# Contiguous halves instead of interleaved chunks of rows in a row-normalising kernel

## The chip, the cores and the metric

One core of a Trainium2 chip; the other cores are idle. The metric is device microseconds (us) of one execution. "Span" is the time from the first to the last instruction in the profile; the time metric lies some 1.7 to 1.8 us above it. Engines: VectorE (DVE), ScalarE (ACT), GpSimd (POOL), SyncE (SP, which here only issues DMAs), and 16 DMA engines that carry every transfer.

## The reference

```python
# x: [1024, 4096] float32, axis = -1, eps = 1e-12
norm = np.sqrt(np.sum(x ** 2, axis=axis, keepdims=True) + eps)
return (x / norm).astype(np.float32)
```

Each row is divided by its own length. A row is 16 KiB, the tensor 16.78 MB; it is read once and written once. No row depends on another, so the kernel is free to give any row to any partition.

## The kernel before

Two tiles, each 128 partitions x 4 rows x 4096 floats (64 KiB per partition, 8.39 MB in all). Both loads are issued at once, then each tile is squared and summed, scaled in place and stored. All four DMAs go through SP's queue.

```python
R = 4
n_tiles = N // (P * R)                       # 2
x_t = x.rearrange("(p t r) d -> t p (r d)", t=n_tiles, r=R)
out_t = out_flat.rearrange("(p t r) d -> t p (r d)", t=n_tiles, r=R)
...
for i in range(n_tiles):
    ...
    load = nc.sync.dma_start(out=g.flat(), in_=x_t[i])
    ...
for i, g in enumerate(groups):
    g.square_dve(R - 1)          # sum of squares of row 3 on VectorE
    g.square_act(0)              # of row 0 on ScalarE
    g.norm(0)                    # sqrt on ScalarE, reciprocal on VectorE
    g.scale(0)                   # x *= 1/norm on VectorE
    ...
    store = nc.sync.dma_start(out=out_t[i], in_=g.flat())
```

Partition p holds rows 8p to 8p+7: rows 8p..8p+3 in tile 0 and rows 8p+4..8p+7 in tile 1. In either tile a partition's four rows are one contiguous run of 64 KiB in HBM, and the runs of neighbouring partitions begin 128 KiB apart.

Of the kernel before, what the change touches and what calls it, by code (L numbers as in the profile page):

```python
# [82 lines left out]
def first_load_to_front(nc, load):  # L83






    def move(program):  # L90
        blocks = program.main_func.blocks
        entry = blocks[0].instructions
        if any(i.name == load.name for i in entry):
            return
        body = next(
            b.instructions
            for b in blocks
            if any(i.name == load.name for i in b.instructions)
        )
        at = next(n for n, i in enumerate(body) if i.name == load.name)  # L100
        assert not body[at].sync_info.on_wait
        before = next(
            n
            for n, i in enumerate(entry)
            if i.engine == mybir.EngineType.SP and isinstance(i, mybir.InstDrain)
        )
        entry.insert(before, body.pop(at))

    nc.at_finalize(move)
# [72 lines left out]
@with_exitstack  # L182
def kernel(
    ctx: ExitStack,
    tc: tile.TileContext,
    x: bass.AP,
    axis: bass.AP,
    eps: bass.AP,
    out: bass.AP,
):  # L190
    nc = tc.nc
    P = nc.NUM_PARTITIONS

    assert isinstance(axis, int) and axis in (-1, len(x.shape) - 1)
    eps = float(eps)

    x = x.flatten_outer_dims()
    out_flat = out.flatten_outer_dims()
    N, D = x.shape
    R = 4  # L200
    assert N % (P * R) == 0
    n_tiles = N // (P * R)
    x_t = x.rearrange("(p t r) d -> t p (r d)", t=n_tiles, r=R)
    out_t = out_flat.rearrange("(p t r) d -> t p (r d)", t=n_tiles, r=R)

    io = ctx.enter_context(tc.tile_pool(name="io", bufs=n_tiles))
    scratch_pool = ctx.enter_context(tc.tile_pool(name="scratch", bufs=1))
    stats = ctx.enter_context(tc.tile_pool(name="stats", bufs=n_tiles))

    eps_t = scratch_pool.tile([P, 1], F32)  # L210
    nc.vector.memset(eps_t, eps)  # L211
    sq_act = scratch_pool.tile([P, D], F32)
    sq_dve = scratch_pool.tile([P, D], F32)
    scratch = {"act": sq_act, "dve": sq_dve}

    groups = []
    for i in range(n_tiles):
        g = RowGroups(nc, io, stats, scratch, D, R, eps_t)
        load = nc.sync.dma_start(out=g.flat(), in_=x_t[i])
        if i == 0:  # L220
            first_load_to_front(nc, load.ins)
        groups.append(g)

    for i, g in enumerate(groups):
        g.square_dve(R - 1)
        g.square_act(0)
        g.norm(0)
        g.scale(0)
        g.square_act(1)
        g.norm(1)  # L230
        g.norm(R - 1)
        g.scale(1)
        g.scale(R - 1)
        g.square_act(2)
        g.norm(2)
        if i < n_tiles - 1:
            g.scale_by_both(2)
        else:
            g.scale(2)
        store = nc.sync.dma_start(out=out_t[i], in_=g.flat())  # L240
    gpsimd_waits_for_last_store(nc, store.ins)
# [35 lines left out]
```

## Time and profile before

| | before |
|---|---|
| time, median of 3 runs | 81.94 us (81.75 to 81.99) |
| span in the profile | 80.2 us |
| DVE / ACT busy | 26.7 / 29.7 us |
| DMA packets | 512 of 64 KiB, 64 completion signals |
| first and second load landed | 22.08 / 41.40 us |

The lines behind the table are shown in the prediction.

### The profile page before, as it was taken

The numbers are of one execution on the slowest core, as the hardware profiler recorded it, in microseconds if no ns is written. First come the engines' busy times: TensorE is split into PE (matmuls) and PEld (weight loads), VectorE is DVE, ScalarE is ACT, GpSimd is POOL, SyncE is SP. The second block draws the span as 40 slices with busy tenths as digits, with TensorE's granted clock in tenths as the row PEclk, the third lists the DMA queues.
The fourth block names the chain that finished last, engine by engine and source line by source line (L and its number), as shares of the span: only waits on it lengthen the run. The fifth ranks groups of instructions, "written<-read, shape, count | busy, mean of one in ns | idle before, by whom it ended". The sixth has DMA issues, their size and how long they took to land.

```text
span 80.2 us, 93 instructions
## 1 busy us (share of the span) xinstructions
DVE 26.7 (33%) x21; ACT 29.7 (37%) x23; POOL 0.2 (0%) x4
## 2 busy tenths in 40 slices
DVE  0000000000099599960039995999200000000000
ACT  6000000000099999989439999950000000000000
POOL 0000000000000000000000000000000000000000
DMA  9099996699996699996699990999991999992990
GB/s 490 33 523 523 523 490 294 261 523 523 523 490 261 294 523 523 523 490 261 294 523 523 523 490 33 523 523 523 523 458 65 523 523 523 523 425 98 523 523 0
DMA packets 576, 33.55 MB, mean 418 GB/s; under 512 B 64, under 2 KB 64, under 8 KB 64
## 3 DMA queue, kind: packets, MB, share of 16 engines
q1 hardware_dynamic: 576, 33.55, 97.4%
HBM read 16.78 MB, written 16.78 MB: 418 GB/s over the span
## 4 chain that ended last, share of the span: by engine, by line
DMA 51%; ACT 10%; DVE 9%; issue 0%
DMA xt<-in_x_dram 51%; ACT sq_act L33 9%; DVE xt L64 9%; ACT rstd L53 1%; DVE rstd L59 0%
## 5 line engine op out<-in xcount | busy, mean ns | idle before, releaser
L33 ACT ACTIVATE sq_act<-xt 128x4096 f32<-128x4096 f32 x6 | 21.7, 3609 | 22.4 <-DMA xt<-in_x_dram 22.4
L42 DVE SCALAR_TENSOR_TENSOR sq_dve<-xt 128x4096 f32<-128x4096 f32 x2 | 8.9, 4426 | 26.4 <-DMA xt<-in_x_dram 26.4
L64 DVE TENSOR_SCALAR xt<-xt,rstd 128x4096 f32<-128x4096 f32 x7 | 16.5, 2353 | 0.2
L72 ACT ACTIVATE xt<-xt,rstd 128x3584 f32<-128x3584 f32 x1 | 3.3, 3283 | 0.2 <-DVE rstd L59 0.2
L53 ACT ACTIVATE rstd<-ssq,eps_t 128x1 f32<-128x1 f32 x8 | 2.1, 290 | 0.1
L59 DVE RECIPROCAL rstd<-rstd 128x1 f32<-128x1 f32 x8 | 1.3, 160 | 2.5 <-ACT rstd L53 2.5
L33 ACT ACT_TABLE_LOAD x1 | 1.3, 1283 | 0.8 <-PEq L258 0.8
L53 ACT ACT_TABLE_LOAD x1 | 1.3, 1283 | 0.0
L33 ACT ACTIVATION_READ_ACCUMULATOR sq_act<-xt 128x1 f32 x6 | 1.1, 187 | 0.0
L78 DVE TENSOR_SCALAR xt<-xt,rstd 128x512 f32<-128x512 f32 x1 | 0.5, 487 | 0.0
L211 DVE MEMSET eps_t<- 128x1 f32 x1 | 0.1, 59 | 0.9 <-PEq L258 0.9
L42 DVE DVE_READ_ACCUMULATOR sq_dve<-xt 128x1 f32 x2 | 0.2, 83 | 0.0
L258 POOL MEMSET const-uint8-127<- 128x1 uint8 x1 | 0.1, 103 | 0.0
L258 POOL MEMSET const-bfloat16-1.0<- 128x1 bf16 x1 | 0.1, 102 | 0.0
L258 POOL MEMSET const-float32-0.0<- 128x1 f32 x1 | 0.1, 99 | 0.2 <-issue 0.2
L258 POOL MEMSET const-float32-1.0<- 128x1 f32 x1 | 0.1, 99 | 0.0
## 6 DMA issues: line engine op xcount, KB each, us to landing
xt<-in_x_dram SPq DMA_DIRECT2D x2, 31.3
out_dram<-xt SPq DMA_DIRECT2D x2, 22.5
```

Of the source, the lines that this page charges most:

```text
L33: self.nc.scalar.activation(out=sq_a, in_=self.x[:, r], func=ACT_F.Square, accum_out=self.ssq[:, r : r + 1],)
L42: self.nc.vector.scalar_tensor_tensor(out=sq_v, in0=self.x[:, r], scalar=1.0, in1=self.x[:, r], op0=ALU.mult, op1=ALU.mult, accum_out=self ...
L53: self.nc.scalar.activation(out=self.rstd[:, r : r + n], in_=self.ssq[:, r : r + n], func=ACT_F.Sqrt, bias=self.eps_t,)
L59: self.nc.vector.reciprocal(out=self.rstd[:, r : r + n], in_=self.rstd[:, r : r + n])
L64: self.nc.vector.tensor_scalar_mul(out=self.x[:, r], in0=self.x[:, r], scalar1=self.rstd[:, r : r + 1])
L72: self.nc.scalar.activation(out=self.x[:, r, :cut], in_=self.x[:, r, :cut], func=ACT_F.Copy, scale=rstd,)
L78: self.nc.vector.tensor_scalar_mul(out=self.x[:, r, cut:], in0=self.x[:, r, cut:], scalar1=rstd)
L211: nc.vector.memset(eps_t, eps)
L258: nc = _bacc.Bacc("TRN2", target_bir_lowering=False, num_devices=1)
```

## The change

The intent, as far as the edit shows it: each tile becomes one contiguous 8 MiB half of the tensor, so that a load or store walks through HBM without leaving every second 64 KiB out.

```diff
-    x_t = x.rearrange("(p t r) d -> t p (r d)", t=n_tiles, r=R)
-    out_t = out_flat.rearrange("(p t r) d -> t p (r d)", t=n_tiles, r=R)
+    x_t = x.rearrange("(t p r) d -> t p (r d)", p=P, r=R)
+    out_t = out_flat.rearrange("(t p r) d -> t p (r d)", p=P, r=R)
```

That is the whole diff. Partition p now holds rows 4p..4p+3 in tile 0 and rows 512+4p..512+4p+3 in tile 1.

## The prediction

> **What bounds the kernel now.** I start with the page of the kernel before: busy engines, the slices, the queue and the chain that ended last.
>
> ```profile
> DVE 26.7 (33%) x21; ACT 29.7 (37%) x23; POOL 0.2 (0%) x4
> ...
> DMA packets 576, 33.55 MB, mean 418 GB/s; under 512 B 64, under 2 KB 64, under 8 KB 64
> ...
> q1 hardware_dynamic: 576, 33.55, 97.4%
> ...
> DMA 51%; ACT 10%; DVE 9%; issue 0%
> ```
>
> VectorE and ScalarE are busy for a third of the 80.2 us span, while packets on the 16 DMA engines fill 97.4% of it. 576 packets are 512 large ones plus 64 tiny ones (the "under 512 B" count): 33,554,432 bytes / 512 = 65,536 bytes, so each large packet is exactly one partition's four rows of 16 KiB. The 64 tiny ones are 16 for each of the four transfers, which are the completion signals. The row of tenths in the slices, with its sixes and zeros, should not be read as idle DMA: a packet takes longer than a 2 us slice, so whole packets fall into one slice or the next. The chain of waits says DMA 51% only, but it ends at the last compute instruction (54.38 + 2.35 = 56.7 us), not at the last store. So it does not show what sets the end. The timeline does:
>
> ```profile
> 0.00 1.12 SPq L219 DMA_DIRECT2D xt<-in_x_dram  x2
> ...
> 22.08 3.62 ACT L33 ACTIVATE sq_act<-xt 128x4096 f32<-128x4096 f32 x1 [20.01 <-DMA xt<-in_x_dram]
> ...
> 38.99 18.11 SPq L240 DMA_DIRECT2D out_dram<-xt  x2
> 41.40 3.62 ACT L33 ACTIVATE sq_act<-xt 128x4096 f32<-128x4096 f32 x1 [2.43 <-DMA xt<-in_x_dram]
> ```
>
> Load 1 has landed at 22.08 us and load 2 at 41.40. The two loads lie in one queue one behind the other, so the second one alone cost 41.40 - 22.08 = 19.32 us for 8,388,608 bytes: 434 GB/s. The stores were issued at 38.99 and about 56.8 us. The view of the output tensor gives their times to landing:
>
> ```profile
> DMA to landing us min/median/max: 21.7/22.5/23.3
> ```
>
> That puts them at 38.99 + 21.7 = 60.7 and 56.8 + 23.3 = 80.1 us. The four landings are at 22.1, 41.4, 60.7 and 80.1, evenly 19.3 us apart: loads and stores cost the same, and nothing lies between them. Windows cut where each transfer ends confirm it (columns: stretch in us, its length, busy time of DVE, ACT, POOL, clock, DMA share, GB/s):
>
> ```profile
> 1.00:20.66 19.66, 0.00 (x0) 1.07 (x1) 0.00 (x0) 1.00 1.02 427
> 20.66:40.00 19.34, 12.45 (x10) 16.56 (x12) 0.00 (x0) 1.00 1.00 434
> 40.00:59.35 19.35, 14.23 (x10) 11.88 (x10) 0.00 (x0) 1.00 1.00 434
> 59.35:78.70 19.35, 0.00 (x0) 0.00 (x0) 0.00 (x0) 1.00 1.00 434
> ```
>
> So the span is one DMA pipe: about 1.0 us before the first packet, then 78.7 - 1.0 = 77.7 us of packets, then 80.2 - 78.7 = 1.5 us until the last completion is seen and the program ends. The packet records say the same from below: nearly all large packets take 2.42 us, each engine moves 32 of them, 32 x 2.42 = 77.4 us. Only the first packet of each engine is longer, 2.4 to 3.4 us with a mean of 3.07: 0.65 us of start-up. The time outside the span is 81.94 - 80.2 = 1.7 us (the profiled execution itself took 82.04), and the change cannot touch it.
>
> **What the Trainium skill says.** "DMA: Bandwidth & Descriptors", section "Where 436 GB/s comes from", puts the ceiling of the 16 engines' SBUF ports at 435.2 GB/s (16 ports x 32 B x 850 MHz). The trace agrees closely: 434 GB/s in three windows, 99.7% of it. "HBM Reference", section "Specifications (TRN2)", has a domain at about 716 GB/s, and adds that a core streaming alone is bounded by its 16 engines; the equal speed of loads and stores fits that, though no run so far measures HBM by itself. Against the change stands a row of the first page, section "Latency and other measured facts", on HBM row pitch at large powers of two: tiles of 128 x 16 KiB copied between HBM tensors made 207 GB/s at a pitch of 512 KiB, 164 at 2 MiB and 103 at 4 MiB, against 214 for a padded pitch. The kernel before has a pitch of 128 KiB between partitions and shows no loss at all; the change halves the pitch, which is the harmless direction of that row. Last, the same page's "Why a DMA increments its semaphore by 16 and not by 1" says the slowest dimension of both patterns decides the number of engines, and 128 gives 16; the 16 completions per transfer in the page above agree.
>
> **The change, part by part.** Only two address patterns change. I built both kernels and compared instruction order: every engine has the same rows (DVE 21, ACT 17, SP 5), with the same waits. In the built program each of the four transfers is, on the HBM side, 128 runs of 16,384 floats; the step from one run to the next goes from 32,768 floats (128 KiB) to 16,384 (64 KiB), and the second tile's offset from 64 KiB to 8 MiB. The SBUF side is untouched.
>
> - Removed: nothing. Added: nothing. Compute is 0 us of difference: the reductions go over one row whichever row it is.
> - Bytes: 2 x 16.78 MB both ways, difference 0.
> - Packets: still 128 runs of 65,536 bytes per transfer. The run was already contiguous, because a partition's four rows lie together in both layouts. So contiguity of the whole tile joins no packets, as a packet cannot cross from one SBUF partition to another. 512 x 0 us saved.
> - Speed of a packet: at 434 of 435.2 GB/s (a figure of the skill) the most that a friendlier HBM order could give is 77.4 x 0.3% = 0.2 us (estimate). The start-up could give at most its 0.65 us. The whole upside is under 0.9 us, 1.1%.
> - Compute overlap: from landing 1 to the issue of store 1 it is 38.99 - 22.08 = 16.9 us, against 19.3 us of load 2. Store 1 is thus queued about 1 us before load 2's last packets end (40.0 us). Nothing here depends on which row it is.
>
> Sum: 0.0 us, so 81.9.
>
> **The rivals.**
> 1. *A contiguous 8 MB tile is faster in HBM* (fewer pages open, neighbouring streams). This is the change's evident intent. Against it: HBM isn't what limits, since reads and writes both run at the port ceiling. It would make 81.1 us at the very best, by the sum above, and so cannot be a verdict of faster.
> 2. *The new pitch collides in HBM.* The engines work at the same time on runs whose distance is a power of two, and halving it might bring them onto the same channels. Against it: 128 KiB shows none of it, and the skill's row gets worse with larger pitch only. If it cost 5% of a packet, 77.4 x 0.05 = 3.9 us, giving about 86 us. I give it one chance in twenty-five.
> 3. *The contiguous source is cut up anew* when descriptors are made: one long run of 8 MB instead of 128 runs, with other packet sizes or fewer engines. The built instruction still has the two-dimensional pattern, which speaks against it. If packets became shorter (say 4 KiB) the time might rise by a few per cent; fewer engines would double it.
> 4. *Store 1 comes late.* It is queued only about 1 us before the loads end. If load 1 landed late against load 2 a gap would open. With the landing spacing fixed by the queue I see no reason, and a 0.3 us shift would cost at most 0.3 us.
>
> **Range and chances.** The three timed runs before spread from 81.75 to 81.99 us, and the profiled one took 82.04. I put the median at 81.9 and let the range span that spread with some 0.3 us on either side: 81.6 to 82.3. Faster by over 2% (below 80.3) would need more than the 0.9 us that exist: 0.01. Slower by over 2% (above 83.6) comes from rivals 2 and 3 only: 0.04. Within 2%: 0.95.
>
> **What would show it.** In the profile after: again 576 packets with 64 under 512 B, the queue at about 97%; the first ScalarE square of tile 1 at 22.1 and that of tile 2 at 41.4 us, 19.3 apart; windows at 434 GB/s. If rival 1 holds, the first landing moves below 21.9 or the windows reach 435. If rival 2 holds, the landings are wider apart than 19.4 us with the same number of packets, perhaps in loads or stores alone. If rival 3 holds, the packet count changes. If rival 4 holds, the landings of loads stay and only the stores' move. The prediction is wrong if HBM's order matters at a rate at which the ports are already full, which this trace of one layout cannot exclude.

## The result

The changed kernel takes 81.88 us (median of 6 runs, 81.70 to 82.06) against 81.94 us before (6 runs, 81.72 to 82.02). The ratio is 1.000, 95% interval 0.998 to 1.002; it is the mean time of the changed kernel's fast runs over that of the fast runs of the kernel before in the same rounds, so not quite the ratio of the medians. The result is correct.

The page of the changed kernel, the lines that answer to those of before:

```profile
DVE 26.7 (33%) x21; ACT 29.7 (37%) x23; POOL 0.2 (0%) x4
DMA packets 576, 33.55 MB, mean 420 GB/s; under 512 B 64, under 2 KB 64, under 8 KB 64
q1 hardware_dynamic: 576, 33.55, 97.6%
```

The number and size of the packets are the same, and so is the busy time of each engine. Its timeline (start, length, engine, line, instruction; in brackets the idle time before it and what ended it):

```profile
21.75 3.62 ACT L33 ACTIVATE sq_act<-xt 128x4096 f32<-128x4096 f32 x1 [19.68 <-DMA xt<-in_x_dram]
38.64 18.13 SPq L240 DMA_DIRECT2D out_dram<-xt  x2
41.07 3.62 ACT L33 ACTIVATE sq_act<-xt 128x4096 f32<-128x4096 f32 x1 [2.45 <-DMA xt<-in_x_dram]
```

The second load took 41.07 - 21.75 = 19.32 us: to the hundredth what it took before. Everything is 0.33 us earlier than in the first profile of the kernel before, from the first landing on. Its windows:

```profile
20.66:40.00 19.34, 12.45 (x10) 16.54 (x12) 0.00 (x0) 1.00 1.00 434
40.00:59.35 19.35, 14.23 (x10) 11.87 (x10) 0.00 (x0) 1.00 1.00 434
59.35:78.70 19.35, 0.00 (x0) 0.00 (x0) 0.00 (x0) 1.00 1.00 434
```

434 GB/s in loads and stores alike, as before. So the question for the experiments is not where time went, but why the order of addresses in HBM costs nothing, and for which other orders that holds.

### The profile page after: what moved, and what is told of

It reads as the page before. It is cut to its first block, busy times and chain, and to the rows that moved or that the text cites. A ratio compares the mean times of both kernels' runs of the same rounds, so it can differ in the third digit from the quotient of the medians.

```text
span 79.9 us, 93 instructions
## 1 busy us (share of the span) xinstructions
DVE 26.7 (33%) x21; ACT 29.7 (37%) x23; POOL 0.2 (0%) x4
## 4 chain that ended last, share of the span: by engine, by line
DMA 50%; ACT 10%; DVE 9%; issue 0%
DMA xt<-in_x_dram 50%; ACT sq_act L33 9%; DVE xt L64 9%; ACT rstd L53 1%; DVE rstd L59 0%
```

## The experiments

**Theory P**: the 16 DMA engines move 64 KiB packets at their own pace (2.42 us each, loads and stores); HBM has room to spare, so the order of the packets in HBM cannot show. What can show is the number of packets, by a fixed cost of each. **Rival H**: the order in HBM does matter, and the two layouts of the change are merely both harmless ones. (An "order" here is the distance in HBM between the runs of neighbouring partitions, and between the pieces of one partition.) A smaller question came up on the way: is the 0.33 us of the first landing the change's doing?

### The changed kernel and the kernel before once more

No edit; both kernels again, five rounds for the changed one and one look at the one before.

> The changed kernel once more. In its first profile the first load landed 0.34 us earlier than in that of the kernel before (first packets 2.91 us on the mean, not 3.07). If the contiguous order makes the start faster, the ratio is below 1 by 0.3 us / 81.9 us = 0.4% with an interval clear of 1, and the first landing is at 21.7 us again. If it is the scatter of one profile, the ratio is 1.000 within 0.2% and the first landing anywhere from 21.6 to 22.2 us.

> The kernel before once more, for a second profile of its start. Scatter: a first landing off the earlier 22.06 us by some tenths. Layout effect: 22.0 to 22.1 us again.

Measured: 81.97 us (6 runs) against 81.87 us (11 runs), ratio 1.0011, interval 0.9996 to 1.0027. The single run of the kernel before took 81.90 us. First landings of the second profiles, the changed kernel and then the one before:

```profile
21.91 3.62 ACT L33 ACTIVATE sq_act<-xt 128x4096 f32<-128x4096 f32 x1 [19.84 <-DMA xt<-in_x_dram]
```

```profile
21.93 3.62 ACT L33 ACTIVATE sq_act<-xt 128x4096 f32<-128x4096 f32 x1 [19.86 <-DMA xt<-in_x_dram]
```

21.91 and 21.93 us: the 0.33 us were the scatter of single profiles. (The first two profiled executions took 82.04 us before and 81.70 us after, the two ends of the spread.) The packet records say where that scatter sits. The first packet of each engine took 3.07 us on the mean in the first profile of the kernel before and 3.09 in the second; in the two of the changed kernel 2.91 and 3.11. Later packets took 2.42 us on the mean. The means alone don't put the landings in order; the slowest engine does, since a load has landed when its last packet has. Load 1's last packet ended at 21.72 and 21.57 us in the two profiles of the kernel before, at 21.38 and 21.54 in those of the changed one.

### Every partition reads the same run

The step between partitions is zero, so all 128 partitions read one run of 64 KiB; loads only. Whether this is the worst order for HBM no run shows. The result is wrong.

```diff
-        load = nc.sync.dma_start(out=g.flat(), in_=x_t[i])
+        load = nc.sync.dma_start(out=g.flat(), in_=x_t[i][0:1].broadcast_to([P, R * D]))
```

> Wrong result on purpose: in both loads every partition reads the same 64 KiB run of HBM (a step of zero), stores as before. [...]Theory P as I put it in the prediction says only that harmless orders are hidden by the ports; if it holds in its strong form (no order at all matters) the loads still take 19.3 us each and the time is 81.9 us. Rival H: 16 engines on one place collide and each load takes well over 20 us (say 25 to 40), the time 90 us or more, while the two stores stay at 19.3 us.

Measured: 82.03 us (4 runs), ratio 1.0015 (1.000 to 1.003). The timeline:

```profile
21.70 3.62 ACT L33 ACTIVATE sq_act<-xt 128x4096 f32<-128x4096 f32 x1 [19.64 <-DMA xt<-in_x_dram]
41.28 3.62 ACT L33 ACTIVATE sq_act<-xt 128x4096 f32<-128x4096 f32 x1 [2.71 <-DMA xt<-in_x_dram]
```

The second load took 41.28 - 21.70 = 19.58 us, 0.26 more than in either layout of the change; its packets took 2.442 us on the mean instead of 2.419. So with 16 engines on one 64 KiB run this load loses 1.3%. Rival H, which expected 25 to 40 us, falls for this order. The strong form of theory P, no effect at all, is off by those 0.26 us.

### The same packets in other orders: runs of 16 KiB

Here a partition's four rows come from separate places, so a packet is one row, and there are four times as many. Three orders with the same packet size; the results are correct.

```diff
-    x_t = x.rearrange("(t p r) d -> t p (r d)", p=P, r=R)
+    C = 4096
+    x_c = x.rearrange("n (k c) -> (n k) c", c=C)
+    x_t = x_c.rearrange("(a t p) c -> t p a c", t=n_tiles, p=P)   # near: neighbours 16 KiB apart
+    # mid:  "(a p t) c -> t p a c"                                # neighbours 32 KiB apart
+    # far:  "(p a t) c -> t p a c"                                # neighbours 128 KiB apart
     ... (the output in the same way; the tile viewed as "p r (k c) -> p (r k) c")
```

> Correct result. A partition's four rows now come from four places 4 MiB apart, and neighbouring partitions are 16 KiB apart, on loads and stores: 2,048 packets of 16 KiB in place of 512 of 64 KiB. Theory P (the DMA engines' own pace at the SBUF ports sets the time, and the order in HBM does not matter): a packet costs its bytes plus at most 9 ns (65,536 bytes at the skill's 435.2 GB/s for 16 engines would be 2,409 ns, measured 2,418), so four 16 KiB packets cost at most 27 ns more than one of 64 KiB, 32 x 27 ns = 0.9 us: 81.9 to 82.8 us, transfers 19.3 to 19.5 us apart. Rival H (the order in HBM matters, and both layouts of the change merely happen to be harmless): off by more than 1% from the far variant with the same packets.

> Correct result. The same 2,048 packets of 16 KiB, but neighbouring partitions 128 KiB apart and a partition's four rows at a step of 32 KiB (every second row of its eight). Theory P: equal to the near variant within 0.3%, 81.9 to 82.8 us. Rival H: near and far differ by over 1%, one of them at 83 us or more.

> Correct result. 16 KiB packets with neighbouring partitions 32 KiB apart (twice near) and the same 4 MiB step between a partition's rows; its HBM pattern keeps the form of near (128 runs by 4), where far had become one list of 512 runs. The far variant issued its first load 0.24 us longer (677 ns, near 433 ns) and its packets began 0.36 us later. If that is the form of the pattern, mid is as near: first issue 430 ns, first packet at 1.1 us, 82.3 us. If it is the distance in HBM, mid is between the two: 82.4 to 82.6 us.

Measured: near 82.28 us (ratio 1.0050, 1.003 to 1.007), mid 82.23 (1.0044, 1.003 to 1.006), far 82.66 (1.0093, 1.008 to 1.011), four runs each. Near and far differ by 0.4%, a little more than theory P allowed and far less than rival H needs. The timelines, near and then far:

```profile
0.00 1.21 SPq L222 DMA_DIRECT2D xt<-in_x_dram  x2
...
21.90 3.62 ACT L33 ACTIVATE sq_act<-xt 128x4096 f32<-128x4096 f32 x1 [19.78 <-DMA xt<-in_x_dram]
...
41.49 3.62 ACT L33 ACTIVATE sq_act<-xt 128x4096 f32<-128x4096 f32 x1 [2.71 <-DMA xt<-in_x_dram]
```

```profile
0.00 1.90 SPq L222 DMA_DIRECT2D xt<-in_x_dram  x2
...
22.41 3.62 ACT L33 ACTIVATE sq_act<-xt 128x4096 f32<-128x4096 f32 x1 [19.81 <-DMA xt<-in_x_dram]
...
42.00 3.62 ACT L33 ACTIVATE sq_act<-xt 128x4096 f32<-128x4096 f32 x1 [2.71 <-DMA xt<-in_x_dram]
```

The second load takes 19.59 us in both (41.49 - 21.90 and 42.00 - 22.41). The whole difference, 0.5 us, lies before the first landing and starts in the first line: issuing the two loads ended at 1.21 us for near and at 1.90 for far. The view of the load's line gives the length of one issue (minimum, median, maximum, in ns), near, mid and far:

```profile
L222 SPq DMA_DIRECT2D xt<-in_x_dram x2: 372/402/433, 0.0 to 0.8; - x2
```

```profile
L222 SPq DMA_DIRECT2D xt<-in_x_dram x2: 372/400/429, 0.0 to 0.8; - x2
```

```profile
L222 SPq DMA_DIRECT2D xt<-in_x_dram x2: 574/626/677, 0.0 to 1.3; - x2
```

Far needs up to 0.24 us longer to issue, and by the packet records its first packet began at 1.46 us, not 1.10 (near) or 1.09 (mid). In the built programs the far pattern had been folded into one list of 512 equally spaced runs, while near and mid kept 128 runs by 4. That this form costs the time is the likely reading: the difference is already there while SP issues. Mid, at twice near's distance, showed no step towards far. The kernel before speaks against the distance too: its neighbours are as far apart as far's, 128 KiB, in 128 runs of 64 KiB, and issuing its loads took no longer than issuing near's:

```profile
L219 SPq DMA_DIRECT2D xt<-in_x_dram x2: 333/358/383, 0.0 to 0.8; - x2
```

But no run has far's distance with 16 KiB packets in near's form, so the cause stays argued, not shown.

### Smaller runs: 4 KiB and 1 KiB

If order shows at all, I expected it with small pieces. The edit is the one above with C = 1024 and C = 256 and the near and far orders. A partition then gathers pieces of several rows, so the norms mix rows: wrong. (The comparison passed all the same, within its tolerance; random rows of 4096 have almost equal norms. They are no valid kernels for other data.)

> Wrong result on purpose (a partition gathers pieces of several rows, so the norms mix rows; bytes and instructions are the same). Pieces of 4 KiB, neighbouring partitions 4 KiB apart, a partition's sixteen pieces per 64 KiB at a step of 1 MiB. From the runs so far a packet costs its bytes at 2,409 ns per 64 KiB plus a fixed 9 ns on stores (64 KiB 2,418, 16 KiB 611) and some 13 ns on loads (16 KiB 615). So theory P (fixed cost per packet, order in HBM hidden) expects 151 + 9 = 160 ns on stores and 164 on loads, transfers of 20.4 and 20.9 us, about 87 us. Rival H: something else, and another value than the far variant by over 1%.

> Wrong result on purpose, as the near variant, with neighbouring partitions 128 KiB apart and a partition's pieces at a step of 8 KiB. Theory P: as near, about 87 us, but for the start, where the 16 KiB far variant began its first packet 0.36 us later than near (and its first packets were 0.3 us longer): up to 0.8 us more. Rival H: over 1 us apart from near in transfers 2 to 4.

> Wrong result on purpose. Pieces of 1 KiB, neighbours 1 KiB apart, a partition's pieces at a step of 256 KiB. Theory P: 38 + 9 = 47 ns on stores, 51 on loads, 64 of them per 64 KiB: 3.0 and 3.2 us, transfers of 23.9 and 25.9 us, about 104 us if nothing new appears[...]. Rival H: near and far over 1% apart.

> Wrong result on purpose. Pieces of 1 KiB, neighbours 128 KiB apart, a partition's pieces at a step of 2 KiB. Theory P: as near, about 104 us, to 1%. Rival H: over 1% apart in transfers 2 to 4.

Measured, four runs each: 4 KiB near 84.92 us (ratio 1.038), far 85.51 (1.045); 1 KiB near 97.48 (1.191), far 98.32 (1.201). The timelines of 4 KiB near, then of 1 KiB, near and far:

```profile
22.75 3.62 ACT L33 ACTIVATE sq_act<-xt 128x4096 f32<-128x4096 f32 x1 [20.64 <-DMA xt<-in_x_dram]
43.19 3.62 ACT L33 ACTIVATE sq_act<-xt 128x4096 f32<-128x4096 f32 x1 [3.58 <-DMA xt<-in_x_dram]
```

```profile
0.00 20.12 SPq L222 DMA_DIRECT2D xt<-in_x_dram  x2
...
26.07 3.62 ACT L33 ACTIVATE sq_act<-xt 128x4096 f32<-128x4096 f32 x1 [23.95 <-DMA xt<-in_x_dram]
50.11 3.62 ACT L33 ACTIVATE sq_act<-xt 128x4096 f32<-128x4096 f32 x1 [7.17 <-DMA xt<-in_x_dram]
```

```profile
26.96 3.62 ACT L33 ACTIVATE sq_act<-xt 128x4096 f32<-128x4096 f32 x1 [24.35 <-DMA xt<-in_x_dram]
50.92 3.62 ACT L33 ACTIVATE sq_act<-xt 128x4096 f32<-128x4096 f32 x1 [7.09 <-DMA xt<-in_x_dram]
```

Near and far again differ before the first landing only (26.07 against 26.96 us); the second load takes 24.04 and 23.96 us. For 4 KiB the first landings are 22.75 and 23.29, the second loads 20.44 and 20.45 us. In these loads order is hidden at every size tried, and the size is not. The second load divided by its packets per engine:

| run in HBM | packets per engine | second load, us | ns per packet | bytes at 435.2 GB/s, ns | over, ns | GB/s |
|---|---|---|---|---|---|---|
| 64 KiB (both layouts) | 8 | 19.32 | 2415 | 2409 | 6 | 434 |
| 16 KiB | 32 | 19.59 | 612 | 602 | 10 | 428 |
| 4 KiB (near) | 128 | 20.44 | 160 | 151 | 9 | 410 |
| 1 KiB (near) | 512 | 24.04 | 47 | 38 | 9 | 349 |

(435.2 GB/s is the figure of the Trainium skill, "DMA: Bandwidth & Descriptors", section "Where 436 GB/s comes from", so the column "over" is an estimate.) A packet of a load costs its bytes plus 6 to 10 ns. Without the skill's figure, from one row to the next, each further packet added 11, 9 and 9 ns. SP's issuing doesn't set this pace: issuing both 1 KiB loads had ended at 20.12 us, before the first packet of load 2 at 25.30 by the records.

For stores the 9 ns are not a constant. The page of 1 KiB near has the GB/s in 40 slices of 2.4 us; by the packet records store 1 runs from 49.4 to 71.1 us and store 2 from there to 95.1:

```profile
GB/s 153 368 350 347 347 349 350 348 347 348 348 349 348 348 347 349 349 348 347 347 357 388 386 387 386 386 388 385 388 386 380 347 348 348 347 350 347 349 348 247
```

Store 1 moves some 386 GB/s, which is about 5 ns over its bytes per packet, store 2 some 348 as the loads do (estimates of the same kind). The far variant shows the same two rates. Why the two stores differ stays open.

The small runs show one thing more. In the near orders neighbouring partitions follow each other in HBM without a gap, as they do in the changed kernel, and still each packet is one piece of one partition: 8,192 packets of 4 KiB besides the 64 signals.

```profile
DMA packets 8256, 33.55 MB, mean 404 GB/s; under 512 B 64, under 2 KB 64, under 8 KB 8256
```

My expectations of 87 and 104 us were too long because I had added up the durations of packet records. The records of neighbouring packets overlap: in the 1 KiB near run they sum to 101.4 us per engine within a span of 95.6 us. The distance between landings is the safer measure.

### Copies within one memory

Two runs ask what paces a packet at 2.42 us. In the first, load 2 is replaced by a copy of tile 1 inside SBUF; in the second, load 2 and store 2 by one copy from HBM to HBM. Half the rows are wrong.

```diff
-        load = nc.sync.dma_start(out=g.flat(), in_=x_t[i])
+        load = nc.sync.dma_start(out=g.flat(), in_=x_t[i] if i == 0 else groups[0].flat())   # SBUF copy
```

```diff
+        if i == 1:                                                                           # HBM copy
+            nc.sync.dma_start(out=out_t[i], in_=x_t[i])
+            continue
```

> Wrong result on purpose for half the rows: the second load is replaced by a copy of the first tile inside SBUF (it waits for load 1). HBM is not read in it at all. Theory P: the same 128 packets of 64 KiB at the same 2.42 us each, so landing 19.3 us after it starts, plus 2 to 3 us for the wait and the issue (time 84 to 87 us, as the scaling of tile 1 has to wait for the copy, more: up to 100). Rival H (HBM sets the 2.42 us): another packet time without HBM reads, 10% or more away.

> Wrong result on purpose for half the rows: in place of load 2 and store 2, one copy from HBM to HBM of the same 128 runs of 64 KiB. It touches HBM twice per byte and SBUF not at all. If the DMA engines' own pace sets 2.42 us and HBM has room (theory P), packets stay at 2.42 us, the copy lands at 41.4 us and the time is about 62.6 us. If HBM is what limits (rival H), the copy's packets are up to twice as long, 4.8 us, and the time about 82 us.

Measured, one run each, so of unknown state: 104.14 and 68.29 us. Both expectations missed: neither copy kept 2.42 us. In the HBM copy only its first 16 packets did; the mean was 3.09 us. The DMA views (tensors, sequencer, count, us from issue to landing), SBUF copy and then HBM copy:

```profile
xt<-in_x_dram SPq DMA_DIRECT2D x1, 21.9
xt<-xt SPq DMA_DIRECT2D x1, 32.6
```

```profile
xt<-in_x_dram SPq DMA_DIRECT2D x1, 21.9
out_dram<-in_x_dram SPq DMA_DIRECT2D x1, 46.2
```

The HBM copy was issued at 0.79 us behind load 1, so it landed at 47.0, 25.1 us after load 1: 8.39 MB / 25.1 us = 334 GB/s read and as much written, 668 GB/s of HBM traffic. The kernel asks HBM for 434. So HBM, with runs 128 KiB apart, can carry more in total than the kernel takes. That it has room in one direction is not shown: the copy read 334 GB/s, less than the 434 that a load reads. The SBUF copy, issued at 21.93 us with its first packet at 23.10 by the records, moved its bytes in 31.4 us: 267 GB/s each way, 534 GB/s of SBUF traffic, its packets 3.78 us long. Each memory thus carries more in total, though not in either direction, than a load or a store asks of it. What exactly holds a packet at 2.42 us (the path of one engine, its port, or the sum of both ends) these two runs do not separate; it stays open, and with it the part of theory P that says HBM has room to spare. That the orders tried change a load by 1.3% at most while the size of the runs is kept, the other runs show.

## Why the prediction was right

**The bound, and the sum of 0.0 us, held.** The second load took 19.32 us in both layouts, the windows show 434 GB/s in both, and the packets are the same 512 of 64 KiB. The measured time is 81.88 us where 81.9 was expected. The reason given, that HBM doesn't limit because loads and stores run at the ceiling of the ports, was not shown: 434 against the skill's 435.2 GB/s is an agreement of two numbers, and the two copies left open what sets the pace.

**"Contiguity of the whole tile joins no packets" held**: 576 packets before and after. The experiments show it to be the point that carries the result. Packets don't join across partitions even where the runs touch in HBM (8,192 packets of 4 KiB in the near order). In the orders tried a layout acts through the length of the run that one partition owns, some 9 ns per packet of a load; with 8 packets of 64 KiB per engine that is nothing.

**Rival 1 (a contiguous tile is faster)**: none seen, ratio 1.000 and then 1.001. The prediction's own sign of it, a first landing below 21.9 us, did appear (21.75), but was gone in the second profile (21.91): the sign was set inside the scatter.

**Rival 2 (the new pitch collides)**: no. Pitches of 1 to 128 KiB at smaller sizes of run showed no collision either, and a pitch of zero, another case, cost 0.26 us in a load. An even pitch over 128 KiB was not tried, and doesn't fit 128 partitions into this tensor. For stores the orders tried are the two layouts and those of the near, mid and far variants; the pitch of zero was a load only.

**Rival 3 (the source is cut anew)**: no, the packet count stayed. That its direction was right for other layouts the runs of 4 KiB show: +3.8%.

**Rival 4 (store 1 comes late)**: the verdict was right, its size wrong. I wrote that store 1 is queued "about 1 us before load 2's last packets end (40.0 us)". The 40.0 was a window's edge, not an end: by the packet records load 2's last packet ended at 41.05 us, store 1 was issued at 38.99, and its first packet began at 40.48, 1.5 us after the issue. The first engine had run dry at 40.27. So the margin is nothing at all for the engines that finish first, some 0.2 us short, and 0.6 us for the last (41.05 - 40.48). It did no harm because the last engine went on without a break (41.05 to 41.06), and it is that engine that ends last. (The records do not name the engine; ends and starts are matched by their times.) In the first profile of the changed kernel no engine ran dry.

**The tail** was another step of that kind. I put 1.5 us after the last packet (80.2 - 78.7), but the windows view books a packet as a whole and 78.7 was my own cut. The records end at 79.69 us, so 0.5 us remain; my own landing of 80.1 us in the same part should have warned me. Neither slip touched the sum, since the change moved neither term.

## What to carry to other kernels

Ask of a layout change what it does to the contiguous run per partition, not to the tile as a whole: the DMAs of these runs were cut at partitions in every layout, and on one core with the others idle the loads ran at 434 GB/s with 64 KiB runs whether neighbours were 64 or 128 KiB apart, and at 428 when all read one run. In the near orders runs of 16 KiB cost half a per cent, 4 KiB 4%, 1 KiB 19% of this kernel, which is almost all DMA. Read the pace of a transfer from the distance between two landings, and do not take window edges for ends or sums of overlapping packet records for time.

## What the Trainium skill lacked or had wrong

- "DMA: Bandwidth & Descriptors", section "Where 436 GB/s comes from", says that the HBM side (about 358 GB/s) binds transfers between HBM and SBUF and the fabric side (435) those within SBUF. On one core alone the runs show the opposite order: 434 GB/s between HBM and SBUF, and 267 GB/s in each direction for one copy within SBUF (one run). The remark on a core streaming alone in "HBM Reference", which the prediction cites, comes close to the 434 (it has about 425).
- The same page, section "Latency and other measured facts", row on HBM row pitch: it covers copies from HBM to HBM and calls 214 GB/s full. The HBM copy here, with 64 KiB runs at a pitch of 128 KiB, made 334 GB/s in one run. The row says nothing of loads into SBUF, where a pitch of 128 KiB, 64 KiB or zero gave second loads of 19.32, 19.32 and 19.58 us.
- The same page has no table for this chip of rate against run length for DMAs issued from SP. It has one point (408.7 GB/s with 4 KiB rows, beside the iDMA measurements) and, for small descriptors, a fixed overhead of some 3 cycles per packet without a measured time. Second loads here: 434, 428, 410 and 349 GB/s for runs of 64, 16, 4 and 1 KiB, some 9 ns per packet.
- No page found says that the form of the access pattern may change the time to issue a DMA: up to 677 ns for one list of 512 runs, 433 ns for 128 runs by 4. The first packet was 0.36 us later with it. (That the form is the cause is argued here, not shown.)
